# A hybrid decoder block on one core: x2 added by VectorE, g_final spread by a transfer, and an on-chip loop inside a skipped branch

## The chip, the cores and the metric

One core of a Trainium2 chip runs the whole block in one launch. The metric is the device time of an execution in microseconds (us); the kernel before was run three times. All engine and trace times below come from one profiled execution of it.

## The reference, cut to what matters

The input has 256 tokens of 1024 features. The block is a mixer (attention beside a gated delta rule), a mixture of 32 experts of which each token uses two, a per-layer embedding, and a last RMSNorm.

```python
x = x + hybrid_mixer(rmsnorm(x, g_mix), ...)                     # this sum is called x2 in the kernel
x = x + hierarchical_moe(rmsnorm(x, g_ffn), ...)                 # this one x3
ple_gate = sigmoid(rmsnorm(x, g_ple) @ w_ple_gate)
x = x + ple_gate * (p @ w_ple_proj)
return rmsnorm(x, g_final)

# in hierarchical_moe, for each of 32 experts:
hid = silu(t @ w_gate[e]) * (t @ w_up[e])
out = out + gate[:, e:e + 1] * (hid @ w_down[e])
```

## The kernel before

**Experts in units.** The kernel gathers, for each expert, the tokens that chose it, and works on up to 32 of them per expert (fewer in the last units, more in the first). The 32 experts are sorted by how many tokens they have and handled in nine units: the first has four experts, two have two, the other six have four (numbered 0 to 8 here). For one unit TensorE multiplies the gathered tokens (tile `XT`) by `gate` and by `up` weights, turns the hidden part over (`hidT`), multiplies it by the `down` weights into the accumulator tile `dn`, and sends each half of the result, split into a rounded high part `yH` and a rest `yL`, back to the tokens through a 0/1 matrix `C` into four accumulators in PSUM, `sum00` to `sum11` (called `total` in the code; `sum` in the trace).

**Weights in a ring.** A weight tile is 1 MB. Tiles live in a ring of slots (names `ra`, `rb`, `rq`, `rs`, `rc`, `xx` with a number). A slot is free again when TensorE has read its tile for the last time, and only then is the next transfer into it issued: by SP for the first experts, by GpSimd (POOL) as a gather by the sorted order for the others.

**Order.** A planner in Python runs over generators with estimated costs and decides in which order each engine's instructions are written. On the chip each engine then takes its own list strictly in order. VectorE (DVE) takes part with the `yL` subtractions, ScalarE (ACT) with the `yH` casts and with copies out of PSUM.

**x2.** The sum after the mixer is held in two tiles `xH` and `xL` (high part and rest, both `xx` in the trace), laid out as 8 groups of 128 features with the tokens outside. `add_x2` brings it into the four accumulators by eight products with an identity matrix `identr`, each 128 by 512, whose moving operand is read with the feature group inside (a step of 512 bytes from element to element). Later `early_features` copies the four accumulators, now x3 without the last units, into the slot tile that `x3(t)` names (two halves by ACT, two by DVE), transposes them, and so makes the input of the embedding's gate.

**Too many tokens.** `overflow` stands in a branch on a flag: if some expert has more tokens than its places, a loop over 32 experts computes what is left, in four windows of 64 tokens. The flag is zero for this input, so every engine loads it, compares, and jumps over the whole part. In Python the four windows are written out one after the other inside the loop.

**g_final.** `ple_rows` loads the 1024 gains of the last norm into one partition by SP and spreads them to all 128 by two products with a row of ones (accumulator `ga`) and two copies by ACT. They are used in the last stage (`finish` and `finals`).

Of the kernel before, what the change touches and what calls it, by code (L numbers as in the profile page):

```python
# [291 lines left out]
def hybrid_block(tc, x, p_t, w_in, w_o_fox, w_o_delta, w_out, w_gate, w_up, w_down, w_ple_gate,  # L292
# [1064 lines left out]
    total = [[None, None], [None, None]]  # L1357

    def add_x2():
        S.copy(identr, ident)  # L1360
        G.memset(late_slots, -1.0)
        G.tensor_copy(late_slots[:, 0:FEW], K("slots")[:, 0:FEW])
        yield after("cb", 4 * 4)
        for t in range(2):
            for n in range(2):
                for part in (xH, xL):
                    P.matmul(total[t][n], identr, part[:, t, :, n * 64:(n + 1) * 64].rearrange("p k q -> p q k"),
                             start=False, stop=False)
                yield
        tell("x2in")  # L1370

    def weights():
# [278 lines left out]
    def hidden(i, pg):  # L1651
        u = UNITS[i]
        m = 128 // len(u)
        yield after("rows", i + 1)
        yield after("th", i + 1)
        yield after("hT", i)
        yield after("rkp")
        yield lambda: None if using else 0.0
        using.append(i)
        hd = K("w_rt")[:, 0:256]  # L1660
        V.scalar_tensor_tensor(hd, PR.pop((i, "th")), QD[i // 2][1][:, half(i), 1:2], pg, op0=OP.mult, op1=OP.mult)
        tell("hd")
        yield
        yield turn()
        pt = ps_t("ga")[:, 0:256]
        for k in range(2):
            P.transpose(pt[:, k * 128:(k + 1) * 128], hd.rearrange("p (q k) -> p k q", k=2)[:, k], ident)
        using.pop()
        yield
        yield after("grp")  # L1670
        hT = mo.tile([128, 2, 128], F32, name="hidT")
        S.copy(hT.rearrange("p k s -> p (k s)"), pt)
        tell("hT")
        tell("ga")
        names = [f"d{e}" for e in u]
        yield (ring.there(*names) if u[0] < FIRST else ring.arrived((0, 2), *names))
        w = [ring.get(n).rearrange("p (q k d) -> p q k d", q=4, k=2) for n in names]
        if i == UL:
            yield from last_down(hT, names, w)
            return  # L1680
        for n in range(2):
            if u[0] >= FIRST:
                yield ring.arrived(HALVES[n], *names)
            if i < UE:
                yield after("y", 2 * i + n)
                py = ps_t("dn")
            else:
                yield after("zl", 2 * (i - UE))
                yield (turn() if n else after("y", 2 * i))
                py = ps_t(("dn", "ga")[n])  # L1690
            for k in range(2):
                for o in range(len(u)):
                    P.matmul(py[o * m:(o + 1) * m, :].rearrange("p (q d) -> p q d", q=2), hT[:, k, o * m:(o + 1) * m],
                             w[o][:, 2 * n:2 * n + 2, k, :], start=k == 0, stop=k == 1, skip_group_check=True)
            plan.add((parts if i < UE else late_parts)(i, n, py))
        for n in names:
            ring.done(n)
        yield
# [21 lines left out]
    def overflow():  # L1720
# [12 lines left out]
        with tc.If(n > 0):  # L1733
            V.memset(big[:, 0:1], 1.0)
            V.tensor_copy(rg[:, :, 1:2], gr[:, :, 0, 0:1])
            with tc.For_i(0, E) as e:
# [3 lines left out]
                for i, src in ((0, rko), (2, gr[:, :, :, 1])):  # L1740
                    V.tensor_tensor(prod, src, oh, op=OP.mult)
                    V.tensor_reduce(rg[:, :, i:i + 1], prod, axis=AX.X, op=OP.add)
                for win in range(T // 64):
                    for t in range(2):
                        V.tensor_scalar(g[:, t * 64:(t + 1) * 64], K("slots"), float(64 * win), rg[:, t, 0:1],
                                        op0=OP.add, op1=OP.is_equal)
                    for k in range(8):
                        pt = ps_t("ga")
                        m = 0
                        for t in range(2):  # L1750
                            for xp in (xH, xL):
                                P.matmul(pt[:, 0:64], xp[:, t, k, :], g[:, t * 64:(t + 1) * 64], start=m == 0, stop=m == 3)
                                m += 1
                        S.activation(X[:, k, :], pt[:, 0:64], AF.Copy, scale=K("g_ffn")[:, k:k + 1])
                    pc = ps_t("ga")
                    for t in range(2):
                        P.transpose(pc[0:64, t * 128:(t + 1) * 128], g[:, t * 64:(t + 1) * 64].bitcast(F32), ident)
                    S.copy(c[0:64], pc[0:64, 0:T])
                    pt = ps_t("ga")
                    for t in range(2):  # L1760
                        P.matmul(pt[0:64, 0:2], g[:, t * 64:(t + 1) * 64].bitcast(F32), rg[:, t, 1:3], start=t == 0, stop=t == 1)
                    V.tensor_copy(wt[0:64], pt[0:64, 0:2])
                    pt = ps_t("ga")
                    pg = [pt[:, 0:256], pt[:, 256:512]]
                    for j, ww in enumerate((w_gate, w_up)):
                        for kc in range(4):
                            src = ww[bass.ds(e, 1)].rearrange("o (p k) f -> p (o k) f", k=8)[:, 2 * kc:2 * kc + 2, :]
                            wv = w.rearrange("p (k f) -> p k f", k=2)
                            nc.sync.dma_start(wv, src)
                            for k in range(2):  # L1770
                                P.matmul(pg[j][0:64], X[:, 2 * kc + k, :], wv[:, k, :], start=kc == 0 and k == 0,
                                         stop=kc == 3 and k == 1)
                    th, hd = tt_[0:64, 0:256], tt_[0:64, 256:512]
                    S.activation(th, pg[0][0:64], AF.Tanh, scale=wt[0:64, 0:1])
                    V.scalar_tensor_tensor(th, th, 1.0, pg[0][0:64], op0=OP.add, op1=OP.mult)
                    V.scalar_tensor_tensor(hd, th, wt[0:64, 1:2], pg[1][0:64], op0=OP.mult, op1=OP.mult)
                    pt = ps_t("ga")
                    for k in range(2):
                        P.transpose(pt[:, k * 64:(k + 1) * 64], hd.rearrange("p (q k) -> p k q", k=2)[:, k], ident[0:64, 0:64])
                    S.copy(hT, pt[:, 0:128])  # L1780
                    for n_ in range(4):
                        py = ps_t("ga")[:, 0:256]
                        wv = w.rearrange("p (k d) -> p k d", k=2)
                        nc.sync.dma_start(wv, w_down[bass.ds(e, 1)][:, :, n_ * 512:(n_ + 1) * 512].rearrange(
                            "o p (k d) -> p (o k) d", k=2))
                        for k in range(2):
                            P.matmul(py[0:64, :], hT[:, k * 64:(k + 1) * 64], wv[:, k, :], start=k == 0, stop=k == 1)
                        S.copy(yH[0:64], py[0:64])
                        V.tensor_tensor(yL[0:64], py[0:64], yH[0:64].bitcast(F32), op=OP.subtract)
                        for t in range(2):  # L1790
                            for y in (yH, yL):
                                P.matmul(total[t][n_ // 2][:, (n_ % 2) * 256:(n_ % 2 + 1) * 256],
                                         c[0:64, t * 128:(t + 1) * 128], y[0:64], start=False, stop=False, skip_group_check=True)
        return s1, s2

    def crowded():
        yield after("flag")
        yield after("x2in")
        ring.cap -= 2
        yield lambda: ring.free[1][2] if len(ring.free) > 1 else None  # L1800
        yield turn()
# [15 lines left out]
    def ple_rows():  # L1817
# [5 lines left out]
            ple.append(ring.take(F32)[0])  # L1823
        pT = ple[1][:, 0:512].rearrange("p (k t) -> p k t", k=2)
        nc.sync.dma_start(pT, p_t.rearrange("(k p) t -> p k t", p=128))
        gf = ple[1][:, 1024:2048]
        nc.sync.dma_start(gf[0:1, :], bass.AP(tensor=g_final.tensor, offset=g_final.offset, ap=[[0, 1], [1, D]]))
        at = plan.load(plan.end, 1 << 18)
        yield after("group", 3)
        yield ring.there("wpp0")  # L1830
# [11 lines left out]
                yield  # L1842
        ring.done("wpp0")
        tell("pp")

        for n in range(2):
            yield turn()
            ps = ps_t("ga")
            P.matmul(ps, ones[0:1, :], gf[0:1, n * 512:(n + 1) * 512], start=True, stop=True)
            yield  # L1850
            S.copy(gf[:, n * 512:(n + 1) * 512], ps)
            tell("ga")
            yield

# [18 lines left out]
    def room():  # L1875

        yield after("crowd")
        yield after("group", (NU + 1) // 2)
        features.append(mr.tile([128, 2, 8, 128], F32, name="xx0"))
        ring.add(mr, "xx", 1, 2)  # L1880
        yield
# [14 lines left out]
    def x3(t):  # L1896
        return ple[2][:, t * D:(t + 1) * D]

    def early_features(t):

        yield lambda: 0.0 if len(ple) > 2 and features else None
        for n in range(2):
            yield after(f"done{t}", n + 1)
            x = x3(t)[:, n * 512:(n + 1) * 512]
            (V.tensor_copy if n else S.copy)(x, total[t][n])
            yield
            yield turn()
            pt = ps_t("ga")
# [352 lines left out]
```

## Time and profile before

| what | value |
|---|---|
| median of 3 runs | 523.71 us (522.18 to 524.1) |
| profiled execution, its own time | 521.74 us |
| its span, first to last instruction | 519.9 us |
| TensorE busy, share of the span | 476.1 us, 92% |
| VectorE, ScalarE, GpSimd busy | 43%, 39%, 25% |
| mean granted TensorE clock | 0.969 |

The span leaves out what lies ahead of the first and behind the last instruction, 1.8 us here. A busy share is a mean over stages with different limits, and the ends of matmuls are modelled, so a full TensorE in the table is where to start reading, not a verdict.

### The profile page before, as it was taken

Reading aid. Unit: us, or ns where it says so; the run is one execution under the profiler, and the core shown is the slowest. Engines: PE = TensorE matmul, PEld = TensorE weight load, DVE = VectorE, ACT = ScalarE, POOL = GpSimd, SP = SyncE. Lnnn points to the kernel's source line nnn. Section 1 sums busy time; section 2 is a strip of 40 time slices with the busy share of each in tenths; the row PEclk is TensorE's granted clock in tenths of the full one; section 3 lists DMA queues with packets and bytes.
Section 4 is the critical chain, followed back from the end, with each engine's and each line's share of the span. In section 5 each row is a group of like instructions: output and inputs, shape, how many; then the busy total and the mean of one; then the engine's idle time right before and its main releaser. Section 6 shows DMA issues by size and latency. Waiting matters only on the chain. (4 is left out here: it accounts for less than half of the span.)

```text
span 519.9 us, 10333 instructions
## 1 busy us (share of the span) xinstructions
PE 476.1 (92%) x4313; PEld 343.1 (66%) x4313; DVE 223.2 (43%) x532; ACT 202.3 (39%) x465; POOL 127.7 (25%) x153
## 2 busy tenths in 40 slices
PE   7999999999999999998999988867868779989993
PEld 7999998889999999877565544434325444334341
DVE  3888779773646748677232111100011140101146
ACT  5675855657654554424322122121210350100244
POOL 5000461300000000033224443412374363260000
PEclk9999999999999999997999999978989799999998
DMA  8944442222279658986499999999999999960002
GB/s 339 366 166 161 162 167 84 84 83 85 79 296 400 238 200 337 421 319 219 156 422 422 420 421 420 414 418 419 418 348 417 420 412 420 387 242 3 1 0 81
DMA packets 25028, 141.23 MB, mean 272 GB/s; under 512 B 2561, under 2 KB 2833, under 8 KB 11538
## 3 DMA queue, kind: packets, MB, share of 16 engines
q0 software_dynamic: 13744, 82.86, 39.2%
q1 hardware_dynamic: 11090, 57.15, 29.1%
q8 instruction: 35, 0.57, 0.5%
q10 hardware_dynamic: 144, 0.52, 0.3%
q14 instruction: 15, 0.12, 0.1%
HBM read 139.46 MB, written 1.05 MB: 270 GB/s over the span
## 5 line engine op out<-in xcount | busy, mean ns | idle before, releaser
L77 PE MATMUL mm<-hH,ra 128*128 128x256 f32 x624 | 116.4, 285 | 0.0
L77 PEld LDWEIGHTS mm<-hH,ra 128*128 128x128 f32 x624 | 96.1, 189 | 1.5 <-issue 0.3
L77 PE MATMUL mm<-hL,ra 128*128 128x256 f32 x312 | 76.4, 282 | 0.5 <-DVE hL L77 0.5
L77 PEld LDWEIGHTS mm<-hL,ra 128*128 128x128 f32 x312 | 58.8, 189 | 1.4 <-DVE hL L77 0.7
L77 DVE TENSOR_TENSOR ra<-ra,ra 128x1024 fp32r<-128x1024 f32 x39 | 48.1, 1237 | 16.5 <-ACT ra L77 16.4
L77 ACT CAST ra<-ra 128x1024 fp32r<-128x1024 f32 x39 | 40.8, 1053 | 24.0 <-PE mm L77 22.0
L77 PE MATMUL dn<-ra,hidT 128*32 128x512 f32 (+2 forms) x108 | 33.5, 624 | 3.4 <-issue 3.1
L77 POOL CAST xx<-xt 128x1024 fp32r<-128x1024 f32 (+1 forms) x2 | 3.3, 1650 | 126.2 <-ACT td L77 123.6
L77 DVE TENSOR_TENSOR yL<-dn,yH 128x512 fp32r<-128x512 f32 x15 | 10.4, 690 | 53.8 <-ACT yH L77 43.5
L77 PE MATMUL up<-ra,XT 128*32 128x256 f32 (+1 forms) x224 | 30.2, 382 | 0.0
L77 ACT ACTIVATE XT<-ga,kp 128x256 f32<-128x256 f32 (+1 forms) x32 | 12.3, 445 | 38.0 <-PE ga L77 31.8
L77 DVE SCALAR_TENSOR_TENSOR kp<-th,wt,up 128x256 f32<-128x256 f32 x9 | 4.3, 480 | 51.4 <-PE up L77 51.4
L77 PE MATMUL gate<-rq,XT 128*32 128x256 f32 (+1 forms) x176 | 24.6, 383 | 1.7 <-issue 1.6
L77 PE MATMUL up<-rb,XT 128*32 128x256 f32 x144 | 23.9, 381 | 0.5 <-issue 0.3
L77 PE MATMUL gate<-ra,XT 128*32 128x256 f32 (+1 forms) x176 | 24.2, 402 | 0.0
L77 PEld LDWEIGHTS ga<-G,xx 128*128 128x128 f32 x128 | 18.5, 215 | 7.9 <-issue 3.7
L77 PE MATMUL ga<-G,xx 128*128 128x256 f32 (+1 forms) x128 | 20.8, 313 | 2.9 <-ACT XT L77 1.5
L77 ACT CAST yH<-dn 128x512 fp32r<-128x512 f32 x15 | 8.8, 587 | 32.8 <-PE sum L77 19.6
L77 PE MATMUL gate<-rb,XT 128*32 128x256 f32 (+1 forms) x112 | 21.0, 416 | 0.3 <-issue 0.3
L77 PE MATMUL dn<-rb,hidT 128*32 128x512 f32 (+1 forms) x64 | 19.1, 612 | 1.0 <-DVE yL L77 1.0
L77 PEld LDWEIGHTS up<-ra,XT 128*32 128x32 f32 (+1 forms) x224 | 14.7, 115 | 7.7 <-issue 2.3
L77 PE MATMUL dn<-rq,hidT 128*32 128x512 f32 (+1 forms) x40 | 19.5, 753 | 0.3 <-DVE yL L77 0.3
(503 smaller groups left out, 1083.8 us busy)
## 6 DMA issues: line engine op xcount, KB each, us to landing
ra<-in_w_in SPq DMA_DIRECT2D x19, 1024.0 KB, 5.4
ra<-in_w_gate SPq DMA_DIRECT2D x4, 1024.0 KB, 4.8
ra<-in_w_out SPq DMA_DIRECT2D x3, 1024.0 KB
ra<-in_w_down SPq DMA_DIRECT2D x3, 1024.0 KB, 11.3
ra<-in_w_o_fox SPq DMA_DIRECT2D x2, 1024.0 KB, 5.7
rq<-in_w_in SPq DMA_DIRECT2D x2, 1024.0 KB, 11.5
rb<-in_w_up SPq DMA_DIRECT2D x2, 1024.0 KB
rb<-in_w_down SPq DMA_DIRECT2D x2, 1024.0 KB, 15.1
```

The source lines that it names most:

```text
L77: return f(*a, **k)
```

## The change

Four edits. `add_x2` no longer multiplies by the identity: VectorE adds `xH` and `xL` and writes the sum into the tile of x3, in natural order, and `early_features` adds the accumulators to what is there (four adds by VectorE instead of two copies by VectorE and two by ScalarE). The part on `g_final` leaves `ple_rows`; in its place ScalarE's queue issues one transfer that writes all 128 partitions, once the last unit's `hidT` is copied. The four windows in `overflow` become a loop on the chip, in which the wanted rank is lowered by 64 in each pass. The waits that tell the planner when these may come are moved accordingly.

```diff
     def add_x2():
         S.copy(identr, ident)
...
-        yield after("cb", 4 * 4)
+        yield lambda: 0.0 if len(ple) > 2 else None
         for t in range(2):
-            for n in range(2):
-                for part in (xH, xL):
-                    P.matmul(total[t][n], identr, part[:, t, :, n * 64:(n + 1) * 64].rearrange("p k q -> p q k"),
-                             start=False, stop=False)
-                yield
+            V.tensor_tensor(x3(t).rearrange("p (q k) -> p q k", k=8), xH[:, t].bitcast(F32).rearrange("p k q -> p q k"),
+                            xL[:, t].bitcast(F32).rearrange("p k q -> p q k"), op=OP.add)
+            yield
         tell("x2in")
...
         tell("hT")
         tell("ga")
+        if i == UL:
+            nc.scalar.dma_start(ple[1][:, 1024:2048], bass.AP(tensor=g_final.tensor, offset=g_final.offset, ap=[[0, 128], [1, D]]))
         names = [f"d{e}" for e in u]
...
-                for win in range(T // 64):
+                with tc.For_i(0, T // 64):
                     for t in range(2):
-                        V.tensor_scalar(g[:, t * 64:(t + 1) * 64], K("slots"), float(64 * win), rg[:, t, 0:1],
-                                        op0=OP.add, op1=OP.is_equal)
+                        V.tensor_scalar(g[:, t * 64:(t + 1) * 64], K("slots"), rg[:, t, 0:1], None, op0=OP.is_equal)
+                    V.tensor_scalar(rg[:, :, 0:1], rg[:, :, 0:1], -64.0, None, op0=OP.add)
                     for k in range(8):
...
     def crowded():
         yield after("flag")
-        yield after("x2in")
+        yield after("cb", 4 * 4)
...
-        gf = ple[1][:, 1024:2048]
-        nc.sync.dma_start(gf[0:1, :], bass.AP(tensor=g_final.tensor, offset=g_final.offset, ap=[[0, 1], [1, D]]))
...
-        for n in range(2):
-            yield turn()
-            ps = ps_t("ga")
-            P.matmul(ps, ones[0:1, :], gf[0:1, n * 512:(n + 1) * 512], start=True, stop=True)
-            yield
-            S.copy(gf[:, n * 512:(n + 1) * 512], ps)
-            tell("ga")
-            yield
...
     def room():
         yield after("crowd")
+        yield after("x2in")
...
             x = x3(t)[:, n * 512:(n + 1) * 512]
-            (V.tensor_copy if n else S.copy)(x, total[t][n])
+            V.tensor_tensor(x, x, total[t][n], op=OP.add)
```

TensorE's list, between `gate` and `up` of unit 4 (minus is the kernel before, plus the changed one):

```order
 L77 MATMUL gate<-rc_3646,XT 32x256
-L77 MATMUL sum_3512<-xx_2736,identr 128x512
-L77 MATMUL sum_3512<-xx_2737,identr 128x512
 L77 MATMUL ga<-kp,G_2748 128x128 x2
-L77 MATMUL sum_3553<-xx_2736,identr 128x512
-L77 MATMUL sum_3553<-xx_2737,identr 128x512
-L77 MATMUL sum_3513<-xx_2736,identr 128x512
-L77 MATMUL sum_3513<-xx_2737,identr 128x512
-L77 MATMUL sum_3554<-xx_2736,identr 128x512
-L77 MATMUL sum_3554<-xx_2737,identr 128x512
 L77 MATMUL up<-ra_3648,XT 32x256
```

The eight identity products are gone and nothing takes their place on this engine; the two transposes between them stay.

VectorE's list, at the two halves of unit 3's `down` result:

```order
 L77 COPY wt<-ga 128x4
-L77 TENSOR_TENSOR yL<-dn,yH 128x512 x2
+L77 TENSOR_TENSOR yL<-dn,yH 128x512
+L77 TENSOR_TENSOR rb_3885<-xx_2736,xx_2737 128x1024 x2
+L77 TENSOR_TENSOR yL<-dn,yH 128x512
 L77 SCALAR_TENSOR_TENSOR th<-th,gate 128x256
```

The two adds of x2 now stand between the two `yL` subtractions. Their target is a slot of the ring (`rb`, slot 4), whose tile before that is one of the four `down` tiles of unit 3, so the first add waits until TensorE has read it in the second half.

TensorE's list at the branch, before and then changed; after the lines of dots come the end of the skipped part and the place where the jump lands:

```order
L1732 TENSOR_LOAD flag
L1733 COMPARE_AND_BRANCH
L1736 COMPARE_AND_BRANCH
...
L1736 UNCONDITIONAL_BRANCH
L1733 UNCONDITIONAL_BRANCH
L77 MATMUL ga<-kp 128x128 x2
```

```order
L1734 TENSOR_LOAD flag
L1735 COMPARE_AND_BRANCH
L1738 COMPARE_AND_BRANCH
...
L1738 UNCONDITIONAL_BRANCH
L1735 UNCONDITIONAL_BRANCH
L77 MATMUL ga<-kp 128x128 x2
```

The branch and its neighbours stand where they stood. What the dots stand for shrinks from four windows of 78 products to one, with the instructions of one more loop.

## Rows read from the trace of the kernel before

**Rows 1.** Busy time by stretch: five engines, then granted clock, DMA share, GB/s.

```profile
340.00:345.00 5.00, 2.98 (x14) 2.30 (x18) 0.00 (x0) 0.57 (x2) 1.87 (x2) 0.58 1.02 419
345.00:350.00 5.00, 4.69 (x32) 1.59 (x28) 0.69 (x1) 2.00 (x5) 0.00 (x0) 0.74 1.00 416
```

**Rows 2.** POOL's timeline: first gather, last `gate` gather of unit 5, of unit 7.

```profile
253.96 1.07 POOL L209 DMA_INDIRECT ra<-in_w_gate,idx  x1 [7.87 <-PE gate L77]
...
321.82 0.94 POOL L209 DMA_INDIRECT rb<-in_w_gate,idx  x1 [2.98 <-PE dn L77]
...
398.93 0.94 POOL L209 DMA_INDIRECT ra<-in_w_gate,idx  x1 [0.30 <-issue]
```

**Rows 3.** The chain that ended last (start, us, what): `gate` of unit 5, of unit 7.

```profile
358.19 3.41 PE gate L77 x32
...
424.90 4.03 PE gate L77 x64
```

**Rows 4.** TensorE's timeline at the identity products (start, us).

```profile
327.49 1.26 PE L77 MATMUL sum<-xx,identr 128*128 128x512 f32 x2
328.55 0.42 PE L77 MATMUL ga<-kp,G 128*128 128x128 f32 x2
328.72 3.17 PE L77 MATMUL sum<-xx,identr 128*128 128x512 f32 x6
331.82 0.40 PE L77 MATMUL up<-ra,XT 128*32 128x256 f32 x1
```

**Rows 5.** The chain: the two products that spread g_final.

```profile
374.49 1.05 PE ga L77 x2
...
377.41 1.06 PE ga L77 x2
```

**Rows 6.** Line 1733, the branch, by engine's queue: ns min/median/max, first to last start.

```profile
L1733 SPq COMPARE_BRANCH  x1: 45/45/45, 323.4 to 323.4; - x1
L1733 PEldq COMPARE_BRANCH  x1: 6192/6192/6192, 335.0 to 335.0; - x1
```

**Rows 7.** TensorE's timeline around the branch.

```profile
335.41 1.21 PE L77 MATMUL ga<-G,xx 128*128 128x256 f32 x8
341.56 0.67 PE L77 MATMUL ga<-kp 128*128 128x128 f32 x2 [4.94 <-PEq L1733]
```

**Rows 8.** The chain behind the branch.

```profile
342.69 2.08 PE ga L77 x8
344.77 3.35 PE dn L77 x16
...
349.50 1.92 PE dn L77 x16
```

**Rows 9.** VectorE's 128x1024 pass; a plain product; an identity product (ns min/median/max).

```profile
L77 DVE TENSOR_TENSOR ra<-ra,ra 128x1024 fp32r<-128x1024 f32 x39 | 48.1, 1237 | 16.5 <-ACT ra L77 16.4
...
L77 PE MATMUL sum<-yH,C 128*128 128x512 f32 x28 | 12.6, 449 | 0.4 <-ACT yH L77 0.4
...
L77 PE MATMUL sum<-xx,identr x8: 673/689/766, 327.5 to 331.2; 128*128 128x512 f32 x8
```

**Rows 10.** Timeline of TensorE and VectorE at unit 3's second half.

```profile
320.98 0.59 PE L77 MATMUL dn<-rb,hidT 128*32 128x512 f32 x1
...
323.11 0.69 DVE L77 TENSOR_TENSOR yL<-dn,yH 128x512 fp32r<-128x512 f32 x1 [3.52 <-ACT yH L77]
...
324.83 0.40 PE L77 MATMUL sum<-yL,C 128*128 128x512 f32 x1
```

**Rows 11.** ACT's 512 KB transfer (us to landing); last `hidT` copy; g_final's first use.

```profile
xt<-in_x ACTq DMA_DIRECT2D x1, 512.0 KB, 5.0
...
480.69 0.37 ACT L77 COPY hidT<-ga 128x256 f32<-128x256 f32 x1 [11.62 <-PE ga L77]
...
510.36 0.69 DVE L77 TENSOR_TENSOR XT<-dn,ra 128x512 f32<-128x512 f32 x1
```

**Rows 12.** TensorE's timeline in the `gate` product of unit 8.

```profile
465.06 0.39 PE L77 MATMUL gate<-rq,XT 128*32 128x256 f32 x1 [0.81 <-issue]
...
466.48 0.38 PE L77 MATMUL gate<-rq,XT 128*32 128x256 f32 x1 [0.79 <-issue]
```

## The prediction, made blind

> **What bounds the kernel now.** I read the page first: TensorE is busy for 92% of the span, all other engines for less than half. All four edits lie behind 320 us, where the experts run, so I read that stage in windows of 5 us. Its transfers look saturated: DMA share 1.0 and about 419 GB/s in each of these windows, even while TensorE stands still [rows 1]. So either TensorE or the DMA could set the pace, and a saving on TensorE is worth something only if the weights are there first. That is the question to settle.
>
> I settled it by counting. POOL issues 31 gathers of 1 MB from 253.96 to 321.82, and SP two more; the last of them is the fourth `gate` tile of unit 5 [rows 2]. At 419 GB/s one takes 2.50 us, so a queue that starts moving at about 255 has landed the 33rd at about 255 + 33 x 2.50 = 337.5. TensorE comes to this tile's product at 358.19 [rows 3]: the weights lie there for 21 us. The same count gives 317.5 for unit 4's `up` (the 25th), used from 331.82 [rows 4], a lead of 14.3 us. For the last `gate` tile of unit 7, issued at 398.93, I estimate in the same way, from the 378 us at which slots ran short and the queue began anew, an arrival at 409 against a use at 424.90 [rows 2, 3], a lead of 16 us. The DMA is full because TensorE frees slots as fast as it fills them, with 14 us or more of weights in hand. TensorE's list is therefore the bound, and time taken out of it reaches the end as long as the sum stays below these leads. A faster TensorE also frees slots sooner, which keeps the DMA full past 378.
>
> **The change, part by part.** Durations are those of the profiled execution (521.74 us; the median of the three runs lies 1.97 above it).
>
> *Identity products.* The eight stand between the end of `gate` and `up` of unit 4: from 327.49 to 331.82 is 4.33 us, of which the two transposes that stay take 0.42 [rows 4]. Nothing else is waited for there. Saved: 3.9 us; at least 3.2 if only the six in one piece count.
>
> *g_final's products.* Two pieces of 1.05 and 1.06 us in the chain [rows 5]. The first stands inside `up` of unit 5; behind the second, the transposes of `hidT` wait for the same accumulator. Saved: 2.1 us. ScalarE loses two copies that nobody waits for apart from that.
>
> *The transfer for g_final.* Its issue comes behind the copy at 480.69, its first use was at 510.36; the same queue landed 512 KB in 5.0 us [rows 11], and no weights move by then. Cost 0; without the cover it would be 5 us.
>
> *The branch.* On TensorE's queue the compare-and-branch lasts 6192 ns, on SP's 45 [rows 6]. SP also jumps, over four windows with 48 transfers and 48 address instructions. So neither the comparison nor the jump as such is slow; what is long on TensorE is the distance: 312 products, about 830 loads and matmuls, since a plain float32 product shows as two of each and a float32r one as one. The engine ends its last work at 336.62 and goes on at 341.56, 4.94 us idle [rows 7]. [...] In the changed kernel the jump passes over one window and two loop frames, about 260 instructions, near to SP's distance. The trace has no jump of this length on TensorE. The bounds are a stall of nothing (SP's 45 ns) and the one seen; the nearer row in distance is SP's, so I take all 7.2 us as saved.
>
> [...]
>
> *The two adds of x2.* They queue on VectorE ahead of the second `yL` of unit 3 and start only when TensorE has read the slot for the last time, at 320.98 + 0.59 = 321.57 [rows 10]. That `yL` was done at 323.80 and its product began at 324.83. If an add takes *a*, the product slips by 321.57 + 2a + 0.69 - 324.83 = 2a - 2.6. A contiguous pass of this size takes 1.24 us [rows 9]: no slip. But both inputs are read in 512-byte steps. No row shows VectorE doing so; the identity products read the same tiles in the same steps on TensorE, and took 689 ns against 449 for a plain product of that size [rows 9], a factor of 1.53. With it a = 1.9 and the slip is 1.2 us; with twice the contiguous time it is 2.3. I take 1.2.
>
> [...]
>
> *Collecting x3.* VectorE gets four adds of 0.69 us (a 512-wide pass from PSUM [rows 10]) for two copies, ScalarE loses two. VectorE has 1.4 us more to do in a stretch where TensorE's transposes wait for it by turns with ScalarE. I cost it at 0.5, between a gain of 0.5 (ScalarE's next cast comes sooner) and a loss of 1.4.
>
> **Sum:** 521.74 - 3.9 - 2.1 - 4.94 - 2.3 + 1.2 + 0.5 = 510.2 us for an execution like the profiled one, and with the 1.97 us to the median **512.2 us**. Saved are 11.5 us, less than the smallest lead late in the stage (16), and at unit 4 only 3.9 against 14.3.
>
> **The rivals.**
>
> *The branch still waits.* [...] Against it: the distance shrinks to under a third. With the whole stall kept the time is 512.2 + 7.2 = 519.4; with half of it, 516.
>
> *The saving doesn't reach the end,* since the DMA is the bound after all and my count of leads is wrong. For it: the saturated share. Against it: TensorE's gaps in this stage end on other engines, not on weights. Then only the places where the DMA ran short can be gained, some 2 us: 521.5.
>
> *The adds of x2 hold VectorE up,* and it gets slower. The mechanism is the slip above: behind the adds stand `yL`, and with it the products that free the accumulator. With the branch unchanged the rest saves 5.5 us before the slip, so it takes a slip of 8.1 to lose 2.6, that is a = 5.4 us, over four times the contiguous row. Even with that factor the time would be just 526.3. Strided reads of the neighbouring engine show 1.53; I find little for it.
>
> *Where the list is cut.* In unit 8's `gate` TensorE stops twice for 0.8 us with nothing named [rows 12], and works in small groups from there on. If that hangs on the place in the list, the shorter list moves it: some 3 us either way, without changing the sign.
>
> **How the numbers follow.** My forecast, the stall gone: 0.53, with a range of its own from 509 to 515. The branch still waiting, in part or whole (515 to 520): 0.34. Saving lost (within 0.5%): 0.08. Slower by the adds: 0.05. A measurement of this kernel tells about 0.5% from no change, 2.6 us. Faster by more than that: the first two cases, 0.87; same: 0.08; slower: 0.05. For the range I leave out the tail below 508.5 (the stall gone and rows 12 gone too, some 0.06) and what lies above 520 (0.13); 508.5 to 520 holds about 0.8.
>
> **What would show it.** Right: no `sum<-xx,identr` products and `up` of unit 4 about 0.5 us behind `gate`; TensorE's compare-and-branch in tens or hundreds of ns and no gap before the transposes of `ga<-kp`; granted clock at 1.0 behind it; `dn` in 1.9 us. VectorE's two 128x1024 adds from 321.6 us at about 1.9 us each; `gate` of unit 7 some 11 us earlier than 424.90 with no wait for weights ahead of it. Wrong: a compare-and-branch of microseconds; adds of over 2.5 us; new gaps on TensorE that end on a transfer; or, in the last stage, VectorE waiting for g_final at its first use.

## The result

| what | before | after |
|---|---|---|
| median of 20 runs | 523.28 us | 521.22 us (517.44 to 524.77) |
| ratio, with its 95% interval | | 0.995 [0.9931, 0.997] |
| profiled execution, its span | 519.9 us | 518.1 us |

The changed kernel is faster by 2.1 us by the medians and by 2.6 by the ratio, which compares the fast runs of both kernels alone. Forecast were 11.5 us, and the range began at 508.5 and ended at 520.0: the direction was right, the size wrong.

The forecast's two largest savings were made where they had been expected. Line 1735 of the changed kernel is the branch; the row gives ns min/median/max and the start:

```profile
L1735 SPq COMPARE_BRANCH  x1: 45/45/45, 324.9 to 324.9; - x1
L1735 PEldq COMPARE_BRANCH  x1: 353/353/353, 338.5 to 338.5; - x1
```

TensorE's compare-and-branch fell from 6192 to 353 ns [rows 6]. The identity products are gone, too, and `up` starts 0.36 us after the two transposes have started. But new stalls stand around these places. VectorE's and GpSimd's timelines of the changed kernel at unit 3's second half (start, us, engine, what, in brackets the idle time ahead and what ended it):

```profile
323.64 4.68 DVE L77 TENSOR_TENSOR rb<-xx,xx 128x1024 f32<-128x1024 f32 x2 [2.10 <-PE dn L77]
328.22 0.69 DVE L77 TENSOR_TENSOR yL<-dn,yH 128x512 fp32r<-128x512 f32 x1
...
323.77 5.37 POOL L209 DMA_INDIRECT rb<-in_w_gate,idx  x1 [5.29 <-PE dn L77]
```

and TensorE's from there to behind the branch:

```profile
326.43 0.50 PE L77 MATMUL sum<-yH,C 128*128 128x512 f32 x1
328.97 0.50 PE L77 MATMUL sum<-yL,C 128*128 128x512 f32 x1 [2.03 <-DVE yL L77]
...
331.73 0.44 PE L77 MATMUL ga<-kp,G 128*128 128x128 f32 x2
332.09 0.40 PE L77 MATMUL up<-ra,XT 128*32 128x256 f32 x1
...
336.31 0.38 PE L77 MATMUL up<-ra,XT 128*32 128x256 f32 x1 [0.81 <-issue]
...
337.78 0.39 PE L77 MATMUL up<-rq,XT 128*32 128x256 f32 x1 [0.88 <-issue]
...
340.54 0.50 PE L77 MATMUL ga<-kp 128*128 128x128 f32 x2 [0.97 <-ACTq L1735]
```

An add of x2 takes 2.3 to 2.5 us, and TensorE waits 2.03 us for the `yL` behind them, where before it had waited for nothing [rows 10]. At the end of `up` it stops twice with nothing named (0.81 and 0.88 us); with slower products in between, `up` took 2.7 us longer than before. The gap behind the branch fell from 4.94 [rows 7] to 0.97.

The third place is the clock. These windows are the whole stretches at the lower level (a granted clock of 0.50) between 330 and 420 us, first of the kernel before, then of the changed one (stretch, length, busy time of five engines, granted clock, DMA share, GB/s):

```profile
340.80:347.60 6.80, 5.58 (x26) 2.69 (x26) 0.00 (x0) 1.21 (x3) 1.87 (x2) 0.50 1.01 418
357.90:361.30 3.40, 3.40 (x34) 1.38 (x32) 0.00 (x0) 0.37 (x1) 0.00 (x0) 0.50 1.01 417
385.20:388.60 3.40, 3.40 (x18) 1.03 (x11) 0.00 (x0) 0.00 (x0) 2.18 (x3) 0.50 0.97 345
405.70:412.50 6.80, 6.80 (x32) 4.29 (x36) 0.00 (x0) 1.14 (x4) 2.08 (x3) 0.50 1.01 420
```

```profile
341.80:345.20 3.40, 3.40 (x20) 1.86 (x22) 0.00 (x0) 0.84 (x2) 0.93 (x1) 0.50 1.02 402
355.40:358.90 3.50, 3.04 (x26) 1.48 (x30) 0.16 (x1) 0.37 (x1) 0.00 (x0) 0.51 1.01 421
386.20:389.60 3.40, 3.40 (x34) 1.47 (x37) 0.00 (x0) 0.37 (x1) 1.83 (x3) 0.50 1.02 407
399.80:413.50 13.70, 11.41 (x66) 5.59 (x66) 1.51 (x3) 3.61 (x9) 3.73 (x4) 0.50 1.01 422
```

The stretch behind the branch became half as long, as forecast in its direction, but the last one became twice as long: 24.0 us in all against 20.4. TensorE worked for 21.25 us of these against 19.18, at half speed, so the lower level cost about 1.0 us more than before where 2.3 had been put down as saved. These are two single executions; the figures over all runs are given further down.

The chain of the changed kernel (start, us, what) shows where a lead of 6 us was lost:

```profile
356.55 3.01 PE gate L77 x32
...
386.61 5.20 PE gate L77 x64
...
405.16 3.56 PE dn L77 x14
408.72 0.23 PE ga L77 x15
408.94 1.27 issue
410.21 3.52 PE dn L77 x16
...
423.01 3.99 PE gate L77 x64
```

The chain of the kernel before at `gate` of unit 6 and at the second half of unit 6's `down`:

```profile
392.56 3.59 PE gate L77 x64
...
414.28 1.92 PE dn L77 x16
```

`gate` of unit 5 comes 1.6 us sooner than before (358.19 [rows 3]), that of unit 6 comes 6.0 sooner, that of unit 7 only 1.9 (424.90), and 1.8 is what is left at the end. Of the 4.1 us in between, 1.6 went where `gate` of unit 6 ran partly at the lower level (5.20 us against 3.59) and 1.6 where the second half of `down` did (3.52 against 1.92).

### The profile page after: what moved, and what is told of

Same layout as the page of the kernel before. It is cut to its first block, busy times and chain, and to the rows that moved or that the text cites. A ratio compares the mean times of both kernels' runs of the same rounds, so it can differ in the third digit from the quotient of the medians.

```text
span 518.1 us, 10304 instructions
## 1 busy us (share of the span) xinstructions
PE 474.2 (92%) x4301; PEld 342.6 (66%) x4301; DVE 228.3 (44%) x536; ACT 200.1 (39%) x461; POOL 133.2 (26%) x153
## 5 line engine op out<-in xcount | busy, mean ns | idle before, releaser
L77 PE MATMUL gate<-rq,XT 128*32 128x256 f32 (+1 forms) x176 | 26.1, 403 | 0.9 <-issue 0.8
L77 PE MATMUL gate<-ra,XT 128*32 128x256 f32 (+1 forms) x176 | 25.3, 417 | 0.0
L77 PE MATMUL up<-rq,XT 128*32 128x256 f32 x80 | 19.6, 382 | 1.0 <-issue 0.9
```

The lines of the kernel that those rows point to most:

```text
L77: return f(*a, **k)
```

## Where the missing 9.7 us are, from the two traces

Forecast 11.5, found 1.8 between these two executions. Differences of start times on TensorE give the terms:

| term | forecast | found |
|---|---|---|
| ahead of the first edit | 0 | +2.0 |
| adds of x2, slip of `yL` | +1.2 | +2.2 |
| identity products | -3.9 | -3.9 |
| end of `up` of unit 4 | 0 | +2.7 |
| stall at the branch | -4.9 | -4.0 |
| clock, by the work done at the lower level | -2.3 | about +1.0 |
| g_final's products | -2.1 | -2.1 |
| collecting x3: waits of `dn` and `sum` near 380 us | +0.5 | -0.3 |
| what remains up to `gate` of unit 7 | 0 | +0.5 |

The found terms sum to -1.9, the lead at `gate` of unit 7; the last of them is the remainder, and the clock is an estimate from the windows above. The first is no effect of the change: the eight runs on chip 7 below, alike up to there, start the second half of unit 3's `dn` between 320.3 and 322.2 us (the one with a longer start put back by its 8.2). The changed kernel with 321.6 is among them, and the profiled execution of before, with 319.6, was early.

## Experiments

The runs were made on two chips. On the one ("chip 7") the kernel before takes 524 to 525 us, like the runs of the result; on the other ("chip 9") 505. Ratios are to the kernel before, run beside it on the same chip.

**The loop alone.** Before, with only the loop in `overflow`.

```diff
-                for win in range(T // 64):
+                with tc.For_i(0, T // 64):
...
```

> The kernel before with only the four windows of the skipped part turned into a loop on the chip. If a shorter jump is worth what the prediction said (the whole 4.94 us gap and 2.3 us of clock behind it), the time is about 7 us under that of before, 516. Theory 1, from the changed kernel's trace: the compare-and-branch falls to some 350 ns and the gap to about 1 us, but TensorE loses 1 to 3 us to small stalls in `up` ahead of it and more at the lower clock later, so 1 to 3 us under before, 520 to 522. Theory 2, that the adds of x2 ate the gain in the changed kernel: about 5 us under before, 518, with no stalls ahead of the branch.

Chip 7: 520.05 us, ratio 0.9908 [0.9872, 0.9944], or -4.8 us. The branch took 358 ns, the gap 0.97, and the granted clock behind it was 1.00:

```profile
336.00:346.00 10.00, 7.75 (x62) 4.18 (x58) 1.17 (x2) 2.96 (x7) 3.74 (x4) 1.00 1.01 415
```

**No branch at all.** Both kernels with the overflow part left out.

```diff
-        slots = overflow()
+        slots = [ring.take(F32)[1], ring.take(F32R)[1]]
```

> The kernel before without the part for experts with too many tokens, so without flag, comparison and jump (left out; its two slots are still taken and given back). It measures what the branch costs in all. By the prediction's price 7.2 us under before, 516. Theory 1 (time gained ahead of 400 us is partly lost at the lower clock and in stalls behind it): 3 to 5 us under before, 518 to 520. If the stall hardly matters to the end: within 1 us of before.

> The changed kernel without the part for experts with too many tokens (left out), so without flag, comparison and jump. Theory 1 (the shorter jump still costs a gap of 1 us and some 2.6 us of stalls in `up` right ahead of it): 2 to 4 us under the changed kernel, 517 to 519, and no stall in `up` of unit 4. If the stalls in `up` don't come from the branch: about 1 us under the changed kernel, 520, and they stay.

Chip 7: 517.95, 0.9868 [0.9836, 0.9901], or -6.9 us, and 518.55, 0.9863 [0.982, 0.9906]. The first agrees with the forecast's price of the stall, 7.2. The second is 2.7 us under the changed kernel by the time and 4.6 by the ratio, although the stalls in `up` stay, for which about 1 us was expected. Its six runs lie in two groups, 515.4 to 516.6 and 520.5 to 521.4 us, and the trace is of the second, so it doesn't show where the rest comes from. In it, TensorE:

```profile
329.70 0.50 PE L77 MATMUL sum<-yL,C 128*128 128x512 f32 x1 [2.13 <-DVE yL L77]
...
338.50 0.38 PE L77 MATMUL up<-rq,XT 128*32 128x256 f32 x1 [0.81 <-issue]
...
341.22 0.50 PE L77 MATMUL ga<-kp 128*128 128x128 f32 x2 [0.93 <-ACT XT L77]
```

There is no branch, and the gap ahead of these transposes is still 0.93: they wait for ScalarE's copies, and did so under the old stall. So only 4.0 of its 4.94 us were the jump's. The small stalls in `up` are not the jump's either.

**The adds behind the second `yL`.** The changed kernel with one more wait for the planner.

```diff
         yield lambda: 0.0 if len(ple) > 2 else None
+        yield after("y", 4 * 2)
         for t in range(2):
             V.tensor_tensor(x3(t)...
```

> The changed kernel with the two adds of x2 behind the second `yL` of unit 3 on VectorE instead of ahead of it; nothing else moves on TensorE's or GpSimd's list. In the changed kernel's trace the products of that `yL` wait 2.03 us. Theory 2 (the adds held TensorE up): the wait goes, 2 us under the changed kernel, about 519. Theory 1 (what is saved in one place is lost at the lower clock later): the wait goes and the time falls by less than 1 us, 520.5 to 521.5. If the adds then hold up unit 4's `th`: no gain, with a wait of TensorE for `kp` at 337 us.

> The same kernel as adds_late, beside the next one on one chip. It was 1.5% under before (8 us); between 6 and 10 us under before is expected again, with `up` of unit 4 at full pace in the records and still some 2.9 us between the jump and the transposes behind it.

Chip 7, measured twice: 516.23, 0.9846 [0.9798, 0.9893], and 516.45, 0.9838 [0.978, 0.9895], below the interval of the result. No `yL` is waited for, and GpSimd's gather beside the adds took 1.60 us, not 5.37. But 2.9 us stand ahead of the transposes behind the branch (first TensorE, then VectorE, both from the first trace):

```profile
331.95 0.39 PE L77 MATMUL up<-rb,XT 128*32 128x256 f32 x2
...
336.37 0.67 PE L77 MATMUL ga<-kp 128*128 128x128 f32 x2 [2.90 <-ACTq L1736]
```

```profile
335.00 0.48 DVE L77 SCALAR_TENSOR_TENSOR kp<-th,wt,up 128x256 f32<-128x256 f32 x1 [4.87 <-remote]
```

The jump itself took 353 ns here too. But VectorE's `kp`, which reads `up`, starts 2.7 us after the end of `up` in the records, where in the kernel before it started 0.14 after it. So the ends in the records seem too early, and TensorE lost the time at the end of `up` once more. From the start of `up` to `kp` the five traces without the identity products or other work in their place (the changed kernel, with and without the branch, these two, and the moved list below) take 2.4 to 2.6 us longer than the kernel before; the three on chip 7 with the identity products take as long as it does.

In the second trace TensorE comes to `gate` of unit 7 at 411.21 us and waits for the last of its weights:

```profile
412.73 0.63 PE L77 MATMUL gate<-ra,XT 128*32 128x256 f32 x1 [0.44 <-DMA ra<-in_w_gate,idx]
```

The prediction had estimated the arrival of this tile at 409, so the lead over the use at 424.90 was nearer 12 us than 16.

**Dead work in the place of the identity products.** The last kernel with 16 products of 128 by 256 that nobody reads ahead of `up` of unit 4.

```diff
+                if i == 4 and j == 1:
+                    for r in range(16):
+                        nc.tensor.matmul(pu[:, 256:512], identr, xH[...], start=True, stop=True, skip_group_check=True)
```

> adds_late with 16 products of 128 by 256 more (float32r, into columns that nobody reads) between `gate` and `up` of unit 4, where the identity products stood: work of 2.4 us that does nothing. Theory 3, that TensorE runs short of instructions at the end of `up` when `up` follows `gate` without a rest, and that the identity products hid this: the 2.4 us replace the 2 to 3 us that are lost there, so within 1 us of adds_late, and the gap before the transposes falls from 2.9 to about 1 us. Rival, that the loss has another cause: 2.4 us above adds_late and the gap stays.

Chip 7: 523.01, 0.997 [0.9936, 1.0003], 6.6 us above the late adds, where theory 3 had expected 1 and the rival 2.4. The 16 took 2.1 us. The gap ahead of the transposes fell by 1.9 to 0.98, as theory 3 had it, but `up` itself took 1.1 us longer. From the transposes ahead of `up` to those behind the branch it is 9.2 us, against 8.0 and 8.1 with the late adds alone: about half of what the dead products took was free. Behind the branch a new gap cost more (TensorE's timeline):

```profile
338.70 0.50 PE L77 MATMUL ga<-kp 128*128 128x128 f32 x2 [0.98 <-ACTq L1740]
339.66 0.39 PE L77 MATMUL ga<-G,xx 128*128 128x256 f32 x1 [0.46 <-ACT hidT L77]
343.01 1.66 PE L77 MATMUL ga<-G,xx 128*128 128x256 f32 x7 [2.96 <-issue]
```

**The list moved.** The changed kernel with 32 products of one column in its warm-up, so that all behind stands 128 instructions later (each shows as two loads and two matmuls).

```diff
         warm(20)
+        for _ in range(32):
+            nc.tensor.matmul(ps[:, 0:1], ones, ones[:, 0:1], start=True, stop=True)
```

> The changed kernel with 32 products of one column more in the warm-up at the start (64 to 128 instructions, while TensorE waits for its first data anyway), so that all that follows stands later in TensorE's list. If the small stalls depend on where a part stands in the list (the prediction's rival on rows 12), those at the end of `up` of unit 4 and 6 and in `gate` of unit 8 move or go, and the time moves by up to 3 us either way. If they depend on dense work alone (theory 3): the same places, the same length, the time within 1 us of the changed kernel.

Chip 7: 529.17, 1.0055 [1.0019, 1.0091]. The start became 8.2 us longer; less that, the time is the changed kernel's. The small stalls stand where they stood in the program, at the end of `up` of units 4 and 6 and in `gate` of unit 8. So the rival "where the list is cut" falls for them, unless the cuts repeat at just this distance.

**x2 as before, the rest changed.** The identity products and the four copies back in the changed kernel.

```diff
-            V.tensor_tensor(x3(t).rearrange(...), xH..., xL..., op=OP.add)
+            for n in range(2):
+                for part in (xH, xL):
+                    P.matmul(total[t][n], identr, part[...], start=False, stop=False)
```

> The changed kernel with x2 brought in by the eight identity products again and x3 copied as before; the loop on the chip and the transfer for g_final stay. Against loop_only it tells what g_final's two products were worth: by the prediction 2.1 us under loop_only (0.9908 of before), so 0.987 of before. Theory 2 and 3 say that the adds of x2 brought a net loss, so this one is 3 to 4 us under the changed kernel. If the late stage takes the gain of g_final (less time for VectorE and ScalarE there), it is level with loop_only.

Chip 7: 517.73, 0.9869 [0.9824, 0.9915]. Against the loop alone (0.9908) this is g_final's part, about 2.0 us, with intervals that overlap. Against the result (0.995) it says that the edit on x2 as a whole gained nothing and rather cost about 4 us; the two intervals do not touch, though the two kernels were not run side by side.

**The other chip.** The two kernels again, and three ways with x2: dead identity-like products added to the late adds, the adds read contiguously (so the sum has its features in another order), and the adds behind the branch.

```diff
-            V.tensor_tensor(x3(t).rearrange("p (q k) -> p q k", k=8), ...rearrange("p k q -> p q k")
+            V.tensor_tensor(x3(t), ...rearrange("p k q -> p (k q)")
```

```diff
         yield lambda: 0.0 if len(ple) > 2 else None
+        yield after("crowd")
```

> The kernel before, unchanged, for a trace beside the next three on one chip. On a chip on which it takes about 505 us, theory 4 (there the weights set the pace from unit 6 on) wants waits of TensorE in `up` of unit 6 at 379 to 382 us and ahead of `gate` of unit 7 at 410 to 412 us, in spite of the long branch at 335. On a chip on which it takes about 524 us: the known trace, with small stalls of TensorE that nothing names in units 6 and 8.

> The changed kernel itself, unchanged, beside the next three on one chip, since the gaps between the kernels are of the size of what two sessions differ by. It was 0.995 of before (0.993 to 0.997); the same is expected, 2 to 4 us under before.

> adds_late (the two adds behind the second `yL`) with eight products like the old identity products at their old place, written into columns that nobody reads: 4.3 us of work on TensorE that does nothing, and no other change. If the identity products were worth what the prediction said, it is 3.9 us above adds_late (0.984 of before), so 0.9915. Theory 3 (TensorE loses 2 to 3 us at the end of `up` when it follows `gate` without this rest): 1 to 1.5 us above adds_late, 0.987, like identity_back.

> The changed kernel with the two adds of x2 at their place, but reading and writing straight through instead of in steps of 512 bytes (x2 then stands in another order, so what is computed from it changes; the work is the same). If the adds' length at this place is what makes the changed kernel slow: 1.2 us for an add instead of 2.4, no wait of TensorE before the `yL` product, GpSimd's gather at 324 us short again, and the time near that of adds_late, 0.984 to 0.988 of before. If it is the place in VectorE's list whatever the length, or the missing identity products: near the changed kernel, 0.993 to 0.997.

> The changed kernel with the two adds of x2 behind the branch, where VectorE has little to do, ahead of unit 4's first `yL`. If all that matters is that the adds hold no `yL`: like adds_late, 0.984 of before. If VectorE's 4.8 us push unit 4's first `yL` (due some 10 us behind the branch) or hold the four gathers of unit 5's `down`: between adds_late and the changed kernel, 0.987 to 0.993, with longer gathers at 336 to 342 us.

Chip 9, in this order: 505.49, 504.98, 505.87, 505.8 and 505.54 us, ratios 1.0004, 0.9996, 1.001, 1.0002 and 1.0002, each within 0.3% of 1. On this chip no edit gains anything, not even contiguous adds that take 1.2 us each and hold no `yL`. The small unnamed stalls at the end of `up` and in `gate` of unit 8 are absent in these traces, the kernel before among them, so the dead products could not test here what they were meant to test. The branch saves its 4 us here too (6132 ns and a gap of 4.95 before), and the changed kernel comes to `gate` of unit 6 at 374.6 us, 8.6 sooner. Then, in its chain:

```profile
343.82 17.55 DMA rq<-in_w_gate,idx
361.37 20.19 DMA rb<-in_w_up,idx
381.56 0.04 issue
381.60 3.64 PE up L77 x58
...
392.74 19.40 DMA ra<-in_w_gate,idx
412.14 0.04 issue
412.18 6.05 PE gate L77 x58
```

and in that of the kernel before on this chip:

```profile
383.23 3.59 PE gate L77 x64
386.82 3.45 PE up L77 x64
...
413.14 3.59 PE gate L77 x64
```

The last `gate` tile of unit 7 was issued at the same time in both (392.74 and, by GpSimd's timeline of before, 392.67) and was there at 412.14. The kernel before needed it at 413.14: a lead of 1 us, so of 8.6 us only 1 could get past this place. In this execution that went, too: the product ran at a granted clock of 0.59 and took 6.05 us against 3.59. The adds behind the branch, earlier still, wait 1.59, 1.87 and 1.47 us for three tiles of `up` of unit 6.

**The queue relieved.** Two ways to test that. First, the embedding's gate weights, which GpSimd issues ahead of unit 7's `gate`, put behind it; on both kernels.

```diff
-WPG = (7, "g")
+WPG = (7, "u")
```

> The kernel before with the four transfers for the embedding's gate (4 MB) behind those for `gate` of unit 7 instead of ahead of them; the planner then also writes part of the last two units in another order. `gate` of unit 7 should land at about 400 instead of 410 us. On a chip of 505 us TensorE comes to it at 413 in the kernel before, so theory 4 expects no gain from earlier weights here: within 2 us of before, apart from what the new order of the late stage does.

> The changed kernel with the same swap. Theory 4 on a chip of 505 us: TensorE no longer waits at 412 us for `gate` of unit 7, and the time is 2 to 4 us under wpg_before; the waits in `up` of unit 6 at 380 us stay and keep the rest of the gain. If the weights were not what took the gain: no difference to wpg_before. On a chip of 524 us: like the changed kernel against before, 2 to 4 us under wpg_before for other reasons (there it comes to this `gate` at 423).

Chip 9: 507.4, 1.0038 [1.0015, 1.006], against 504.39, 0.9992 [0.997, 1.0015]. The same change is worth 3.0 us now, where it was worth 0.5 or nothing, as expected. The swap alone makes the kernel before 0.4% slower, though, so that both edits together are level with it. The wait ahead of `gate` of unit 7 is gone; the one in `up` of unit 6 stayed:

```profile
380.72 0.41 PE L77 MATMUL up<-rb,XT 128*32 128x256 f32 x2 [1.71 <-DMA rb<-in_w_up,idx]
```

Second, half of the rows of each early unit's `down` weights left out of transfer and product.

```diff
-                    self.rows(t, src, self.index[:, i:i + 1])
+                    h = 64 if name[0] == "d" else 128
+                    self.rows(t[0:h], src, self.index[0:h, i:i + 1])
```

> The kernel before with half of the `down` weights of the experts from the eighth on up to the last early unit left out (64 of 128 rows are gathered and multiplied, so their result is not whole): 12 or 13 transfers of 0.5 instead of 1 MB, some 15 us less for the queue between 255 and 380 us, TensorE's instructions the same in number and length. If TensorE is the bound (the prediction): within 2 us of before. Theory 4, on a chip of 505 us: 3 to 8 us under before, since the waits for weights go and TensorE's own list is left.

> The changed kernel with the same half of these `down` weights left out. It tells what the change is worth where weights are early. Prediction's mechanism: 8 to 12 us under light_before on any chip. Theory 4: so on a chip of 505 us too, where the change itself gives nothing; on a chip of 524 us less, 2 to 6 us, since the stalls by the adds and at the end of `up` stay.

> light_after with the two adds of x2 behind the second `yL` of unit 3. Worth of the adds' place alone where weights are early: 2 us under light_after by the wait in the changed kernel's trace (2.03 us).

Chip 9: 523.57, 514.77 and 517.88 us (1.0373, 1.0191 and 1.0243). It missed its aim: gathers of 64 rows kept the queue as busy and moved less. In this window of the kernel before with half gathers it is 246 GB/s, where the whole ones move 421:

```profile
285.00:300.00 15.00, 15.00 (x156) 8.08 (x152) 2.82 (x8) 2.83 (x8) 6.28 (x7) 1.00 1.03 246
```

TensorE also stood longer at the lower clock (343.4 to 360.5 in the same trace). That the change gains 8.8 us in this pair fits a TensorE that runs some 10 us later and so has leads, but the clock differs as well, so I count it as support only. The late adds were expected ahead of the early ones and came 3 us behind. Their trace shows TensorE waiting for weights in five places, 4.6 us in all, the one with early adds in one, 1.58 us at `gate` of unit 7: here, too, what is saved earlier is lost to the weights.

On chip 7 the late adds lead, with x2 as before inside their interval; they were not run alone on chip 9, where none of the other ways with x2 leads.

## Why the prediction was wrong, step by step

The steps that failed are the two on x2 and the one on the clock; the branch was right but for 1 us.

**The branch: right in mechanism, mis-sized by 1.** The jump no longer waits. Without the branch 6.9 us were gained (interval 5.2 to 8.6), so the price of 7.2 us stood the test; the loop alone gave 4.8 (2.9 to 6.7). What was mis-sized is the gap: 0.9 us of it was a wait for ScalarE that the stall had covered. The first rival falls for the changed kernel. That it was the distance, the loop alone shows (358 ns against 6192); what TensorE waited for, no run does. With the half gathers, though, its jump took 1885 and, with late adds, 1625 ns, so a short jump is not always a quick one; there the time was covered by the wait for ScalarE.

**g_final: right.** 2.1 us in the trace, as forecast; the transfer is not waited for at its first use.

**Identity products: "nothing else is waited for there" failed.** The 3.9 us were saved where they stood, and in the trace of the result 2.7 of them came back within 6 us, in stalls that the profile names only "issue". The branch is excluded, the place in the list too as far as one shift tells. With late adds they stand as one gap, and 16 dead products in the old place took back about 1 us of them, not all. What limits TensorE there stays open; no run shows it.

**The adds: mis-sized.** In all traces 2.3 to 2.5 us each, not 1.9: the factor of 1.53 taken from TensorE [rows 9] was too low, and they came near the upper bound of twice the contiguous row; contiguous they took 1.2. The slip was 2.2, not 1.2. What I missed beside it is GpSimd's gather, held for 5.37 us, until 0.8 us after the end of the adds.

**The clock: the gain didn't come.** The term of 2.3 us, with the gap of 4.94 the price of 7.2, is what the eight gather products (2.08 us against 1.21) and the first half of `down` (3.35 against 1.92) took more behind the branch [rows 7, 8], where the granted clock was 0.58 and 0.74 by windows of 5 us [rows 1]. I booked this low stretch as gone and all others as fixed. In the profiled execution of the changed kernel 24.0 us instead of 20.4 lay at the lower level, so the term was about +1.0 instead of -2.3. Over all runs the median of the mean granted clock is 0.962 before (chip 7) and 0.963 after: no gain either. With the loop alone it is 0.968, without the branch 0.970, with x2 as before 0.968. So the gain was there, and it went with the edit on x2; whether its new waits are the reason, no run shows.

**The leads: right on one chip, wrong on the other.** On chip 7 TensorE comes to `gate` of unit 7 at 417.6 us (no branch) or 417.8 (x2 as before) without waiting for weights, and at 411.2 (late adds) it just waits, 0.44 us. So the lead was some 12 us, not 16, and still enough for 11.5; nor were the transfers full in each window (345 GB/s from 385.2 to 388.6 in the kernel before). On chip 9 the second rival is the truth. The tile lands there at about the same time, 412, but TensorE comes to it 12 us sooner: the kernel before has 1 us in hand at this tile, the saving reaches the waits of `up` of unit 6 and `gate` of unit 7, and nothing is left. The pair with the embedding's weights moved shows it: put the tile's transfer earlier in both kernels and 3 us of difference come through.

## What to carry to other kernels

A saving on the engine that bounds is worth at most the smallest lead that the next tiles have on the slowest queue, counted against the new start times, and on more than one chip where they differ: at `gate` of unit 7 that lead was some 12 us on chip 7 and 1 us on chip 9. Before work is taken out of a dense list, ask what it covered: here a wait of 0.9 us lay under the jump, and on chip 7 some 2.7 us of other stalls appeared once the identity products were gone. New work for a helping engine goes behind the step that the bounding engine waits for, not ahead of it, where that engine is the bound (chip 7, where the adds ahead of it made TensorE wait 2.03 us). A clock gain next to a removed stall is not safe: it came with the loop alone (a median of 0.968 against 0.962) and was gone with the edit on x2 beside it (0.963).

## What was not expected of the hardware

- Two chips run the same kernel in 524 and 505 us; the profiled executions have mean granted clocks of 0.969 and 0.968. The slower one shows small stops of TensorE with nothing named, of 0.81 and 0.79 us in `gate` of unit 8 [rows 12], that the other lacks there.
- GpSimd's issue of a gather, mostly 0.94 us in the kernel before, took 5.37 beside VectorE's two strided adds. In all twelve traces in which one began beside the two adds of x2 it ended 0.8 us after the second, however early it began (3.69 us in the changed kernel on chip 9, 1.46 beside the contiguous adds).
- With gathers of 64 rows among them the transfers moved 246 GB/s where those of 128 rows alone moved 421, with the DMA share at 1.0 both times.
- A jump of about 260 instructions took 353 ns on TensorE, but when the list stood 32 instructions later, the engine stopped for 2.96 us soon behind the landing and went on 6.35 us after the jump, about as long as the old jump's 6.19; with the list 128 instructions later there was no such stop. What it waited for, no run shows.
